# The four pairs of weight buffers of a two-layer encoder at four places modulo 512 bytes

## The chip, the cores and the metric

One core of one Trainium2 chip runs the whole program. The metric is the device time of one execution in microseconds, the less the better. Times before are 2304.95 and 2302.07 us, median 2303.51 us.

## The reference, cut to what matters

An encoder of two layers over 256 tokens of width 2048, all in float32. Layer 0 mixes tokens with gated linear attention, layer 1 with grouped-query attention; each then has a squared-ReLU MLP of width 8192 and a gate by a per-layer embedding.

```python
for i in range(DEPTH):
    u = rms_norm(h, g_pre_mix[i])
    mix = gla_mixer(u, ...) if i % 2 == 0 else gqa_mixer(u, ...)
    h = h + rms_norm(mix, g_post_mix[i])
    m = squared_relu_mlp(rms_norm(h, g_pre_mlp[i]), w_mlp_up[i], w_mlp_down[i])
    h = h + rms_norm(m, g_post_mlp[i])
    gate = sigmoid(h @ w_ple_gate[i])
    h = h + rms_norm(gate * (p[i] @ w_ple_proj[i]), g_ple[i])
```

## The kernel before, in words

Every large product is made in float32r with each operand cut into a high and a low part, and three terms are added up: high by high, high by low, low by high. X (128 partitions, 16 slices of 512 elements) holds the current input, in each slice 256 elements of high parts and then 256 of low parts. H, of the same shape, holds the input of the second product of a stage.

`WeightStream` brings the weights. A chunk is 128 x 1024 float32 (two slices of 128 rows by 512 columns). SP's queue loads it into one of four `raw` buffers, ACT casts it to a high part `whi` (L91), and DVE subtracts to get the low part `wlo` (L92). `whi` and `wlo` have four buffers each (NSPLIT = 4) of 4096 bytes per partition, taken in turn, so the ACT cast of chunk i waits until the matmuls of chunk i - 4 have read its buffer. A few chunks have a destination of their own (`W.dest`) in X, H or a small tile and don't take part in the rotation.

`gemm_b` (L373, L378) makes up, og and the first q and k products: the weights are the stationary operand, X streams. A chunk is 16 matmuls in turn of 512 columns (`whi` against both halves of X) and of 256 (`wlo` against X's high half). `gemm_a` (L300 to L302) makes the others: X or H is the stationary operand and the weights stream, 12 matmuls of 512 columns a chunk: high by `whi`, high by `wlo`, low by `whi`. `gemm_out` is `gemm_a` with its last group of columns in two passes (L339 to L341), the second in matmuls of 256 columns.

Tiles lie one after another in SBUF, in the order in which pools and tags are first used. In the pool `base`: ident (512 bytes per partition), cols, mhalf and ones (512 together), h (16384), X (32768). Then `wpool`: four `raw`, four `whi`, four `wlo`, 4096 bytes each. So modulo 512 all of these lie at X's place, and so does every slice of 128 or 512 elements in them. Then `sm` (small tiles), 19360 bytes up to `mem`, so that the tiles of `mem` (m2 and e4, among them `lrw`, v, qT, kT and prT) lie 416 bytes past X's place modulo 512. Then pools of single stages, and `L1`, which begins with a tile `gap` of 24 floats so that H lies at X's place again; kvlow, PT and other tiles of `L1` follow H.

Of the kernel before, what the change touches and what calls it, by code (L numbers as in the profile page):

```python
# [10 lines left out]
F32 = mybir.dt.float32  # L11
F32R = mybir.dt.float32r
# [5 lines left out]
P = 128  # L18
# [36 lines left out]
CH = KC * 512  # L55


class WeightStream:


    def __init__(self, nc, pool, nraw, nsplit):
        self.nc, self.pool, self.nraw, self.nsplit = nc, pool, nraw, nsplit
        self.chunks = []
        self.raw = {}
        self.split = {}
        self.nload = 0
        self.ndone = 0
        self.pos = 0
        self.on_load = {}
        self.todo = []  # L70
        self.dest = {}
        self.live = 0

    def add(self, ap, kt, n):
        self.chunks.append((ap, kt, n))
# [14 lines left out]
    def _cut(self, hi, lo, raw):  # L90
        self.nc.scalar.copy(hi, raw)  # L91
        self.todo.append(lambda: self.nc.vector.tensor_sub(lo, raw, hi.bitcast(F32)))  # L92

    def parts(self, i):

        kt = self.chunks[i][1]
        return [(k, k + 1) for k in range(kt)] if i == 0 else [(0, kt)]
# [6 lines left out]
    def _split(self, lows=True):  # L104
        i = self.ndone
        _, kt, n = self.chunks[i]
        raw = self.raw.pop(i)
        m = kt * n
        if i in self.dest:
            hi, lo = self.dest[i]  # L110
            if len(hi.shape) == 3:
                self._cut(hi, lo, raw[:, :m].rearrange("p (k n) -> p k n", k=kt))
                self.split[i] = (hi, lo)
                self.ndone += 1
                return
        else:
            hi = self.pool.tile([P, CH], F32R, tag="whi", name=f"whi{i}", bufs=self.nsplit)
            lo = self.pool.tile([P, CH], F32R, tag="wlo", name=f"wlo{i}", bufs=self.nsplit)
            self.live += 1
        for j, k in self.parts(i):  # L120
            self._cut(hi[:, j * n:k * n], lo[:, j * n:k * n], raw[:, j * n:k * n])
        if lows:
            self.lows()
        self.split[i] = (hi[:, :m].rearrange("p (k n) -> p k n", k=kt),
                         lo[:, :m].rearrange("p (k n) -> p k n", k=kt))
        self.ndone += 1
# [24 lines left out]
def kernel(ctx, tc, a, out):  # L151
# [657 lines left out]
        sl = drive(gemm_a(X, 4, v_evac, name="v"), plan, sl)  # L809

    L1 = ctx.enter_context(tc.tile_pool(name="L1", bufs=1))
    L1.tile([P, 24], F32, name="gap")
    H = L1.tile([P, KT, 512], F32R, name="H")

    def load_PT(i):
# [122 lines left out]
    with tc.tile_pool(name="att", bufs=1) as ap_:  # L938
# [166 lines left out]
        for g in range(4):  # L1105
            b = 8 * (g + 1) + ATT_LAG
# [80 lines left out]
```

## Time and profile before

| | us |
|---|---|
| the two runs | 2304.95, 2302.07 |
| their median | 2303.51 |
| the profiled execution | 2302.45 |
| its span, first to last instruction | 2300.7 |
| TensorE busy in the span | 2279.2 |
| VectorE (DVE) busy | 1421.7 |
| ScalarE (ACT) busy | 1215.2 |

Consecutive matmuls overlap in the trace: the time between the starts of two of them is shorter than the duration of one. How fast TensorE goes is therefore read from starts in the timeline, not from durations.

### The profile page before, as it was taken

Reading aid. Unit: us, or ns where it says so; the run is one execution under the profiler, and the core shown is the slowest. Engines: PE = TensorE matmul, PEld = TensorE weight load, DVE = VectorE, ACT = ScalarE, POOL = GpSimd, SP = SyncE. Lnnn points to the kernel's source line nnn. Section 1 sums busy time; section 2 is a strip of 40 time slices with the busy share of each in tenths; the row PEclk is TensorE's granted clock in tenths of the full one; section 3 lists DMA queues with packets and bytes.
Section 4 is the critical chain, followed back from the end, with each engine's and each line's share of the span. In section 5 each row is a group of like instructions: output and inputs, shape, how many; then the busy total and the mean of one; then the engine's idle time right before and its main releaser. Section 6 shows DMA issues by size and latency. Waiting matters only on the chain.

```text
span 2300.7 us, 31255 instructions
## 1 busy us (share of the span) xinstructions
PE 2279.2 (99%) x11956; PEld 1957.1 (85%) x11956; DVE 1421.7 (62%) x1920; ACT 1215.2 (53%) x1884; POOL 37.2 (2%) x58
## 2 busy tenths in 40 slices
PE   8999999999999999999999999999999999999998
PEld 7888888988888888888888888888888888888887
DVE  6888765664564565556667677665455455455565
ACT  6666554654453454455456565555455355355453
POOL 0000000000000000000000010000000000000000
PEclk9999999999999999999999999999999999999999
DMA  8555665665666665666565644666666666666654
GB/s 282 165 147 147 202 192 192 193 191 194 189 189 193 190 191 192 192 190 192 194 215 160 180 143 156 202 187 192 193 191 190 194 187 191 194 190 192 211 174 147
DMA packets 223783, 431.75 MB, mean 188 GB/s; under 512 B 15696, under 2 KB 16720, under 8 KB 222864
## 3 DMA queue, kind: packets, MB, share of 16 engines
q1 hardware_dynamic: 221328, 421.23, 59.5%
q10 hardware_dynamic: 2304, 8.52, 1.0%
q8 instruction: 93, 1.52, 0.3%
q14 instruction: 58, 0.48, 0.1%
HBM read 427.60 MB, written 2.10 MB: 187 GB/s over the span
## 4 chain that ended last, share of the span: by engine, by line
PE 94%; DVE 3%; ACT 1%; issue 1%; DMA 0%; SPq 0%; DVEq 0%; POOLq 0%; POOL 0%; ACTq 0%
PE u L373 20%; PE u L378 11%; PE d L302 9%; PE d L300 9%; PE d L301 9%; PE og L373 3%; PE g L301 2%; PE g L302 2%; PE g L300 2%; PE og L378 1%; PE q L302 1%; PE q L300 1%; PE q L301 1%; DVE wlo L92 1%; PE ao L302 1%
## 5 line engine op out<-in xcount | busy, mean ns | idle before, releaser
L92 DVE TENSOR_TENSOR wlo<-raw,whi 128x1024 fp32r<-128x1024 f32 (+1 forms) x770 | 937.7, 1221 | 731.7 <-ACT whi L91 729.6
L91 ACT CAST whi<-raw 128x1024 fp32r<-128x1024 f32 (+1 forms) x770 | 807.8, 1052 | 842.1 <-PE d L302 338.5
L373 PE MATMUL u<-X,whi 128*128 128x512 f32 x2048 | 711.0, 392 | 0.0
L378 PE MATMUL u<-X,wlo 128*128 128x256 f32 x2048 | 570.9, 280 | 0.0
L373 PEld LDWEIGHTS u<-X,whi 128*128 128x128 f32 x2048 | 383.0, 187 | 83.5
L378 PEld LDWEIGHTS u<-X,wlo 128*128 128x128 f32 x2048 | 386.1, 189 | 0.4
L302 PE MATMUL d<-whi,H 128*128 128x512 f32 x960 | 373.6, 389 | 0.0
L301 PE MATMUL d<-wlo,H 128*128 128x512 f32 x960 | 373.6, 389 | 0.0
L300 PE MATMUL d<-whi,H 128*128 128x512 f32 x960 | 373.4, 389 | 0.0
L302 PEld LDWEIGHTS d<-whi,H 128*128 128x128 f32 x960 | 180.2, 188 | 37.6
L300 PEld LDWEIGHTS d<-whi,H 128*128 128x128 f32 x960 | 180.2, 188 | 37.4
L301 PEld LDWEIGHTS d<-wlo,H 128*128 128x128 f32 x960 | 180.2, 188 | 37.3
L373 PE MATMUL og<-X,whi 128*128 128x512 f32 x256 | 89.6, 396 | 0.0
L300 PE MATMUL g<-whi,X 128*128 128x512 f32 x192 | 75.3, 392 | 0.0
L302 PE MATMUL g<-whi,X 128*128 128x512 f32 x192 | 74.8, 389 | 0.0
L301 PE MATMUL g<-wlo,X 128*128 128x512 f32 x192 | 74.7, 389 | 0.0
L378 PE MATMUL og<-X,wlo 128*128 128x256 f32 x256 | 71.2, 278 | 0.0
L373 PEld LDWEIGHTS og<-X,whi 128*128 128x128 f32 x256 | 48.0, 188 | 11.3
L417 ACT COPY u_c<-u 128x256 f32<-128x256 f32 x128 | 46.8, 366 | 17.5 <-PE u L378 17.5
L373 PE MATMUL q<-X,whi 128*128 128x512 f32 x128 | 46.5, 414 | 6.1 <-ACT whi L91 5.3
L300 PE MATMUL v<-whi,X 128*128 128x512 f32 x128 | 51.3, 401 | 0.0
L300 PE MATMUL q<-whi,X 128*128 128x512 f32 x128 | 50.8, 397 | 0.0
(428 smaller groups left out, 2984.9 us busy)
## 6 DMA issues: line engine op xcount, KB each, us to landing
raw<-in_w_mlp_up SPq DMA_DIRECT2D x256, 512.0 KB, 3.7
raw<-in_w_mlp_down SPq DMA_DIRECT2D x256, 512.0 KB, 3.8
raw<-in_gla_w_in SPq DMA_DIRECT2D x95, 512.0 KB, 4.0
raw<-in_w_ple_gate SPq DMA_DIRECT2D x64, 512.0 KB, 4.2
raw<-in_attn_w_in SPq DMA_DIRECT2D x48, 512.0 KB, 4.1
raw<-in_gla_w_out SPq DMA_DIRECT2D x32, 512.0 KB, 3.9
raw<-in_attn_w_out SPq DMA_DIRECT2D x32, 512.0 KB, 4.4
raw<-in_w_ple_proj SPq DMA_DIRECT2D x7, 512.0 KB, 5.3
```

The costliest lines, as they stand in the source:

```text
L91: self.nc.scalar.copy(hi, raw)
L92: self.todo.append(lambda: self.nc.vector.tensor_sub(lo, raw, hi.bitcast(F32)))
L300: mm(ps[g][t], xh, hi[:, k], start=K == 0, stop=False)
L301: mm(ps[g][t], xh, lo[:, k], start=False, stop=False)
L302: mm(ps[g][t], xl, hi[:, k], start=False, stop=K == nk - 1)
L373: mm(ps[f], hi[:, k, f * P:(f + 1) * P], op[:, K, :], start=K == 0, stop=K == 15, skip_group_check=True)
L378: mm(ps[f][:, T:], lo[:, k, f * P:(f + 1) * P], op[:, K, :T], start=False, stop=K == 15, skip_group_check=True)
L417: nc.scalar.copy(cr[:parts], ps[:parts, T:])
```

## The change

The eight buffers of the rotation get a tag each, with one buffer. A new method `homes` hands them out: pair b = turn modulo 4, where `turn` counts the chunks that take part in the rotation. At its first call it makes all eight in a fixed order, with three tiles in between that nobody writes or reads: 448 bytes, then whi0, wlo1, whi2, wlo2; 64 bytes, then wlo0, whi1, wlo3; 64 bytes, then whi3. Modulo 512 from X's place, (high, low) then lie at (448, 0) for pair 0, (0, 448) for pair 1, (448, 448) for pair 2 and (64, 0) for pair 3. All that lies behind `wpool` moves by 576 bytes. The tile `gap` ahead of H shrinks from 96 to 32 bytes, so H and the tiles behind it move by 512.

```diff
+        self.turn = 0
+        self.first = {}
...
+    def homes(self):
+
+        def new(nm):
+            return self.pool.tile([P, CH], F32R, tag=nm, name=nm, bufs=1)
+        if self.turn == 0:
+            for nm, pad in (("whi0", 448), ("wlo1", 0), ("whi2", 0), ("wlo2", 0),
+                            ("wlo0", 64), ("whi1", 0), ("wlo3", 0), ("whi3", 64)):
+                if pad:
+                    self.pool.tile([P, pad // 4], F32, tag="gap" + nm, name="gap" + nm, bufs=1)
+                self.first[nm] = new(nm)
+        b = self.turn % self.nsplit
+        self.turn += 1
+        return [self.first.pop(nm, None) if nm in self.first else new(nm) for nm in (f"whi{b}", f"wlo{b}")]
...
-            hi = self.pool.tile([P, CH], F32R, tag="whi", name=f"whi{i}", bufs=self.nsplit)
-            lo = self.pool.tile([P, CH], F32R, tag="wlo", name=f"wlo{i}", bufs=self.nsplit)
+            hi, lo = self.homes()
...
-    L1.tile([P, 24], F32, name="gap")
+    L1.tile([P, 8], F32, name="gap")
```

## Rows read from the trace of the kernel before

**Rows 1.** The page: busy time by engine; TensorE's clock in 40 slices, in tenths.

```profile
PE 2279.2 (99%) x11956; PEld 1957.1 (85%) x11956; DVE 1421.7 (62%) x1920; ACT 1215.2 (53%) x1884; POOL 37.2 (2%) x58
...
PEclk9999999999999999999999999999999999999999
```

**Rows 2.** The page: shares of the chain that ended last, by engine.

```profile
PE 94%; DVE 3%; ACT 1%; issue 1%; DMA 0%; SPq 0%; DVEq 0%; POOLq 0%; POOL 0%; ACTq 0%
```

**Rows 3.** Waits of TensorE: who waited for whom, total us, times, longest us.

```profile
PE q L373 <- ACT whi L91: 5.3, 2, 5.2
PE sc L706 <- DVE kcb L699: 3.7, 3, 1.9
PE k L373 <- DVE qk_s L418: 1.9, 1, 1.9
PE xt L426 <- DVE h L457: 0.9, 1, 0.9
PE q L373 <- DVE X L240: 0.8, 1, 0.8
PE v L301 <- DVE wlo L92: 0.2, 1, 0.2
```

**Rows 4.** Timeline, MLP's second product: start us, duration us, what; 16 distances apart.

```profile
1044.68 0.39 PE L300 MATMUL d<-whi,H 128*128 128x512 f32 x1
...
1048.31 0.39 PE L301 MATMUL d<-wlo,H 128*128 128x512 f32 x1
```

**Rows 5.** Timeline, MLP's first product (30 pairs), then the second's first ten distances.

```profile
1025.06 0.39 PE L373 MATMUL u<-X,whi 128*128 128x512 f32 x1
1025.29 0.28 PE L378 MATMUL u<-X,wlo 128*128 128x256 f32 x1
...
1035.45 0.39 PE L373 MATMUL u<-X,whi 128*128 128x512 f32 x1
...
1035.80 0.39 PE L300 MATMUL d<-whi,H 128*128 128x512 f32 x1
...
1038.11 0.39 PE L301 MATMUL d<-wlo,H 128*128 128x512 f32 x1
```

**Rows 6.** Timeline, second pass of the last columns: 19 distances of 256-column matmuls.

```profile
1112.00 0.28 PE L339 MATMUL d<-whi,H 128*128 128x256 f32 x1
...
1114.28 0.28 PE L340 MATMUL d<-wlo,H 128*128 128x256 f32 x1
```

**Rows 7.** Whole span, instructions on whi, then on wlo: PE, PEld, DVE, ACT; clock; DMA.

```profile
0.00:2300.70 2300.70, 2021.00 (x6304) 1173.98 (x6304) 937.65 (x770) 807.82 (x770) 1.00 0.61 188
...
0.00:2300.70 2300.70, 1425.94 (x4432) 835.70 (x4432) 937.65 (x770) 1.00 0.61 188
```

**Rows 8.** Timeline of ACT and DVE in the MLP's second product; idle time and releaser in brackets.

```profile
1044.20 1.05 ACT L91 CAST whi<-raw 128x1024 fp32r<-128x1024 f32 x1 [1.67 <-PE d L302]
1046.92 1.05 ACT L91 CAST whi<-raw 128x1024 fp32r<-128x1024 f32 x1 [1.67 <-PE d L302]
...
1045.29 1.22 DVE L92 TENSOR_TENSOR wlo<-raw,whi 128x1024 fp32r<-128x1024 f32 x1 [1.49 <-ACT whi L91]
```

**Rows 9.** Timeline, attention's output product, six distances of 256-column matmuls.

```profile
1320.82 0.28 PE L1078 MATMUL op<-prT,vn 128*128 128x256 f32 x1
...
1321.52 0.60 PE L1064 MATMUL pp<-ident,pr 128*128 128x128 f32 x4
```

**Rows 10.** Timeline, gate's low-rank product: 16 matmuls in one row, and the next.

```profile
54.89 3.87 PE L772 MATMUL lr<-X,lrw 128*64 128x512 f32 x16
58.60 0.39 PE L373 MATMUL q<-X,whi 128*128 128x512 f32 x1
```

**Rows 11.** Timeline, gated stage's og product: twelve pairs, and six pairs later.

```profile
227.84 0.40 PE L373 MATMUL og<-X,whi 128*128 128x512 f32 x1
...
232.08 0.40 PE L373 MATMUL og<-X,whi 128*128 128x512 f32 x1
...
283.47 0.39 PE L373 MATMUL og<-X,whi 128*128 128x512 f32 x1
...
285.55 0.39 PE L373 MATMUL og<-X,whi 128*128 128x512 f32 x1
```

**Rows 12.** The page: costliest groups, count | busy us, mean ns | idle us before and releaser.

```profile
L91 ACT CAST whi<-raw 128x1024 fp32r<-128x1024 f32 (+1 forms) x770 | 807.8, 1052 | 842.1 <-PE d L302 338.5
```

## The prediction

> **What bounds the kernel now.** I read the page first: busy times, clock and the chain that ended last. [...] Then its waits: together under 14 us in the whole span, nearly all in the first stages [rows 3]. So nothing that feeds TensorE sets the end. What sets it is the distance from the start of one matmul to the start of the next. A duration in a trace can't show that, because consecutive matmuls overlap, so I took starts from the timeline.
>
> In the MLP's second product 16 distances take 1048.31 - 1044.68 = 3.63 us, 226.9 ns each [rows 4]. [...] All of these have every operand at X's place modulo 512: base holds 1024 + 16384 bytes ahead of X, X itself, four raw, four high and four low buffers are multiples of 512, and H has been put there by the 96-byte gap.
>
> The matmuls that read a weight buffer of the rotation are 6304 (high) and 4432 (low), 10,736 together [rows 7]. [...]
>
> **The change, part by part.** *Homes in place of a shared rotation.* The gap tiles are never written and issue nothing; no instruction is added or taken away on any engine or DMA queue. Chunk i took the slot of chunk i - 4, and `turn % 4` gives the same. The ACT cast still waits for the last matmul on the old contents, as now [rows 8]. If separate tags made that wait one chunk longer, there is cover: casts start 1046.92 - 1044.20 = 2.72 us apart, cast and subtraction end 2.27 us after the start of the cast (1.05 us, then DVE at 1045.29 for 1.22), and the buffer is needed three chunks, about 8.2 us, after it came free [rows 8]. That leaves 5.9 us, two chunks. Without that cover each chunk would wait up to 2.3 us; I take 0.
>
> *Cast and subtraction at other addresses.* 1.05 and 1.22 us may move a little; the two together would have to grow beyond the 2.72 us of a chunk on either engine before TensorE notices. 0.
>
> *Everything behind the weight pool moves.* The gaps add 448 + 64 + 64 = 576 bytes, and H's gap shrinks by 64, so H moves by 512 and stays at X's place, with all that follows it in its pool. The small tiles and the work tiles of the attention and the gated stage move by 64 modulo 512. Some 300 matmuls read them; at 5 ns each that is under 2 us. 0.
>
> *The places of the pairs.* Pair 0 has its high half 64 bytes below X's place, pair 1 its low half, pair 2 both, pair 3 its high half 64 bytes above. The trace of before has no weight buffer at such a place. Its nearest rows have operands elsewhere by 96 or 416 bytes. Below: the attention's output product, weights and moving operand at 416, one weight in three at 0: six distances in 1321.52 - 1320.82 = 0.70 us, 116.7 ns [rows 9], 3.3 ns less than the 120.0 of the same shape at equal places. Above: the gate's low-rank product, X streaming against weights at 416 and 160: 16 distances in 58.60 - 54.89 = 3.71 us, 231.9 ns [rows 10], 5.0 ns more than 226.9, though with half the weight columns, so it is not quite the same shape. Over 10,736 matmuls the bounds are -35 and +54 us.
>
> Which value? Both rows are 32 bytes off any 64-byte boundary of X's place (416 = 6.5 x 64), while all the new places are whole multiples of 64. What the rows show may be a matter of such a boundary, which the change does not touch. Also, the spacing depends on more than places: in the gated stage, with the same operands at the same places as in rows 5, twelve pairs take 232.08 - 227.84 = 4.24 us, 353.3 ns a pair instead of 346.3 [rows 11]; and at the switch from the first to the second product the distances wander (the first ten take 1038.11 - 1035.80 = 2.31 us, 231 each) before they hold at 226.9 [rows 5]. A rhythm that settles by itself, at one value through hundreds of matmuls while ACT, DVE and DMA write other buffers, speaks for a fixed turn of access and not for collisions between two particular addresses. I take 0, with both bounds kept for the range.
>
> [...]
>
> *Sum.* 2302.45 us (the profiled execution: 2300.7 of span and 1.75 around it) + 0 = 2302.5, and the median of the runs stands 1.1 us above that execution: 2303 us.
>
> **The rivals.** *B, slower: the rhythm settles anew at each change of pair.* Place: each border between two chunks, about 769 of them (770 casts [rows 12]). Price: the settling above, 2.31 - 10 x 0.2269 = 0.041 us, times 769 = +32 us: 2335 us. For it: the rhythm does depend on where it starts [rows 5]. Against: now a chunk border costs nothing, and 16 equal distances in rows 4 run over one (a chunk has 12). It decides from the point where pairs at different places have different resting phases.
>
> *C, slower: a worse rhythm throughout.* The gated stage's 353.3 ns instead of 346.3 is 3.5 ns per matmul: +38 us, 2340 us; with the 5.0 ns of rows 10 it would be +54, 2356 us. For it: the rhythm of rows 11 holds by itself with nothing amiss on any engine, so a second resting state exists. Against: later in the same stage six pairs take 285.55 - 283.47 = 2.08 us, 346.7 ns each [rows 11]; the dearer rhythm had been left again.
>
> *D, faster: what rows 9 show.* 3.3 ns on all four pairs: -35 us, 2267 us; if half of the pairs gain, 2285 us. For it: rows 9 have mixed places and are the quickest of their shape. Against: six matmuls at a time, which may be settling and not a resting rhythm.
>
> [...]
>
> **How the numbers follow.** A, no change in the spacing: 0.50. B 0.16, C 0.12, D 0.19, E 0.03. A change of over 2% (46 us, about what a measurement of this kernel can tell from no change) needs 4.3 ns on each of the 10,736 matmuls. Slower by that much: a third of C (towards rows 10) and a quarter of B (a settling that takes longer than the one seen), 0.04 + 0.04 = 0.08. Faster by that much: E, and 0.03 of D for places that suit better than those of rows 9: 0.06. Within 2%: 0.86. The likeliest case alone is 2303 us, 2297 to 2309. The range reaches down to rows 9 on all pairs and up to the rhythm of rows 11 on all, 2268 to 2341; outside lie E, 0.03 of D, 0.04 of C and 0.04 of B, and some of the rest at their ends, under 0.2.
>
> **What would show it.** In the changed kernel's timeline the second product should keep 226.9 ns from start to start for each of the four chunks in turn, and the first product 346.3 a pair. [...] The mean durations of these groups, 389 and 392 with 280 ns now, would move with them. The prediction is wrong if a shift of 64 bytes changes which accesses meet: then a period of four chunks appears in the starts. A wait on the new homes would show as TensorE waiting for DVE's or ACT's cast in the MLP stages, where it now waits for nothing.

## The result: 1.1% slower, by the spacing of the matmuls alone

The changed kernel takes 2327.65 us (2326.61 to 2328.69) against 2303.51 us: ratio 1.011, interval 1.0093 to 1.0127. Its span is 2326.9 us, 26.2 us more than before.

The page of the changed kernel, busy time by engine, shares of the chain, and the groups of the MLP's two products (count | busy us, mean ns):

```profile
PE 2305.9 (99%) x11956; PEld 1955.7 (84%) x11956; DVE 1422.7 (61%) x1920; ACT 1212.1 (52%) x1884; POOL 37.2 (2%) x58
...
PE 95%; DVE 3%; ACT 1%; issue 1%; DMA 0%; SPq 0%; DVEq 0%; POOLq 0%; POOL 0%; ACTq 0%
...
L388 PE MATMUL u<-X,whi 128*128 128x512 f32 x2048 | 715.0, 395 | 0.0
L393 PE MATMUL u<-X,wlo 128*128 128x256 f32 x2048 | 570.6, 280 | 0.0
...
L315 PE MATMUL d<-whi,H 128*128 128x512 f32 x960 | 379.2, 395 | 0.0
L316 PE MATMUL d<-wlo,H 128*128 128x512 f32 x960 | 378.2, 394 | 0.0
L317 PE MATMUL d<-whi,H 128*128 128x512 f32 x960 | 378.1, 394 | 0.0
```

Against [rows 1, 2] TensorE is busy 26.7 us longer and idle 0.5 us less, ACT and DVE are busy within 3.1 us of before, and the chain is TensorE's as before. The matmuls of the second product last 394 to 395 ns instead of 389, with no idle time before them.

The waits of TensorE are those of [rows 3], short and in the first stages, and ACT's casts start 2.79 us apart instead of the 2.72 of [rows 8]: they follow TensorE. The changed kernel's longest waits (us in total, times, longest us), then two rows of ACT's timeline:

```profile
PE q L388 <- ACT whi L93: 5.7, 2, 5.4
PE sc L721 <- DVE kcb L714: 2.6, 3, 1.7
PE k L388 <- DVE qk_s L433: 2.0, 1, 2.0
...
1061.07 1.05 ACT L93 CAST whi<-raw 128x1024 fp32r<-128x1024 f32 x1 [1.75 <-PE d L317]
1063.86 1.05 ACT L93 CAST whi<-raw 128x1024 fp32r<-128x1024 f32 x1 [1.74 <-PE d L317]
```

Where the time is shows in starts. A matmul's spacing is the distance from its start to the next one's; in the first product it is given for a pair of matmuls, one of 512 columns (high) and one of 256 (low). From here on each kernel is measured over the same two long stretches: 240 distances within the second product (first quarter of the MLP in layer 0), and 120 pairs within the first product (its second quarter). The timeline of before, then of after (start us, duration us); the last two rows of after are 120 pairs of the first product's last quarter in layer 1:

```profile
517.85 0.39 PE L300 MATMUL d<-whi,H 128*128 128x512 f32 x1
...
572.24 0.39 PE L300 MATMUL d<-whi,H 128*128 128x512 f32 x1
...
615.96 0.39 PE L373 MATMUL u<-X,whi 128*128 128x512 f32 x1
...
657.56 0.39 PE L373 MATMUL u<-X,whi 128*128 128x512 f32 x1
```

```profile
519.61 0.39 PE L315 MATMUL d<-whi,H 128*128 128x512 f32 x1
...
575.36 0.39 PE L315 MATMUL d<-whi,H 128*128 128x512 f32 x1
...
619.85 0.39 PE L388 MATMUL u<-X,whi 128*128 128x512 f32 x1
...
661.97 0.40 PE L388 MATMUL u<-X,whi 128*128 128x512 f32 x1
...
2067.10 0.39 PE L388 MATMUL u<-X,whi 128*128 128x512 f32 x1
...
2108.57 0.39 PE L388 MATMUL u<-X,whi 128*128 128x512 f32 x1
```

Second product: 54.39 us before, 55.75 after, that is 226.6 and 232.3 ns a matmul. First product: 41.60 us before, 42.12 after, 346.7 and 351.0 ns a pair; in the last quarter only 345.6. Summed over all starts of the trace by product, after against before: the second product +15.9 us, the first +4.1, all others together +6.0: 26.0 of the 26.2 us. The +6.0 are +7.3 for the other products with streaming weights, +0.6 for the others with stationary ones, and -1.8 for the rest. The second product's weights stream past H and pay in every quarter, 231.9 to 232.2 ns a matmul there against 226.7; the first product's weights are stationary under X and hardly pay.

### The profile page after: what moved, and what is told of

It is laid out like the page before. It is cut to its first block, busy times and chain, and to the rows that moved or that the text cites. A ratio compares the mean times of both kernels' runs of the same rounds, so it can differ in the third digit from the quotient of the medians.

```text
span 2326.9 us, 31255 instructions
## 1 busy us (share of the span) xinstructions
PE 2305.9 (99%) x11956; PEld 1955.7 (84%) x11956; DVE 1422.7 (61%) x1920; ACT 1212.1 (52%) x1884; POOL 37.2 (2%) x58
## 4 chain that ended last, share of the span: by engine, by line
PE 95%; DVE 3%; ACT 1%; issue 1%; DMA 0%; SPq 0%; DVEq 0%; POOLq 0%; POOL 0%; ACTq 0%
PE u L388 20%; PE u L393 10%; PE d L315 10%; PE d L317 10%; PE d L316 10%; PE og L388 3%; PE g L315 2%; PE g L316 2%; PE g L317 2%; PE q L315 1%; PE og L393 1%; PE q L317 1%; PE q L316 1%; PE k L388 1%; PE go L315 1%; PE ao L315 1%
## 5 line engine op out<-in xcount | busy, mean ns | idle before, releaser
L388 PE MATMUL u<-X,whi 128*128 128x512 f32 x2048 | 715.0, 395 | 0.0
L393 PE MATMUL u<-X,wlo 128*128 128x256 f32 x2048 | 570.6, 280 | 0.0
L388 PEld LDWEIGHTS u<-X,whi 128*128 128x128 f32 x2048 | 384.6, 188 | 87.8
L393 PEld LDWEIGHTS u<-X,wlo 128*128 128x128 f32 x2048 | 384.6, 188 | 0.4
L315 PE MATMUL d<-whi,H 128*128 128x512 f32 x960 | 379.2, 395 | 0.0
L317 PE MATMUL d<-whi,H 128*128 128x512 f32 x960 | 378.1, 394 | 0.0
L388 PE MATMUL og<-X,whi 128*128 128x512 f32 x256 | 89.0, 394 | 0.0
L393 PE MATMUL og<-X,wlo 128*128 128x256 f32 x256 | 71.3, 278 | 0.0
L388 PEld LDWEIGHTS og<-X,whi 128*128 128x128 f32 x256 | 48.1, 188 | 10.7
L388 PE MATMUL q<-X,whi 128*128 128x512 f32 x128 | 46.2, 412 | 6.8 <-ACT whi L93 5.7
```

The costliest lines, as they stand in the source:

```text
L315: mm(ps[g][t], xh, hi[:, k], start=K == 0, stop=False)
L317: mm(ps[g][t], xl, hi[:, k], start=False, stop=K == nk - 1)
L388: mm(ps[f], hi[:, k, f * P:(f + 1) * P], op[:, K, :], start=K == 0, stop=K == 15, skip_group_check=True)
L393: mm(ps[f][:, T:], lo[:, k, f * P:(f + 1) * P], op[:, K, :T], start=False, stop=K == 15, skip_group_check=True)
```

## The experiments

Three theories. **P**: the distance of the weights from X and H modulo 512 sets the spacing. **B**: the rhythm settles anew at each change of pair, and the place itself costs nothing. **H** (a theory here, not the tile): the new homes cost it. Except where a diff says otherwise, a kernel differs from the changed one in the list of gaps (the bytes ahead of each home), and in H's gap, which keeps H at X's place; each diff but one is against the changed kernel, and the two lines that a new list of gaps replaces stand in the first diff only. A ratio is the time over that of the kernel before, run alongside.

**All pairs at (0, 0), with the new homes.**

```diff
-            for nm, pad in (("whi0", 448), ("wlo1", 0), ("whi2", 0), ("wlo2", 0),
-                            ("wlo0", 64), ("whi1", 0), ("wlo3", 0), ("whi3", 64)):
+            for nm, pad in (("whi0", 0), ("whi1", 0), ("whi2", 0), ("whi3", 0),
+                            ("wlo0", 0), ("wlo1", 0), ("wlo2", 0), ("wlo3", 0)):
...
-    L1.tile([P, 8], F32, name="gap")
+    L1.tile([P, 24], F32, name="gap")
```

> Homes as in the changed kernel, but all four pairs at (0, 0), X's place, and H's gap back at 96 bytes. Theory P (the places of the buffers set the spacing of the matmuls): 2303 us within 4, 226.8 ns per matmul in the second product and 346.7 ns per pair in the first, as before. Theory H (a tag and a home for each buffer costs the time, through waits or another order): 2325 to 2330 us, as the changed kernel.

2302.53 us against 2302.32, ratio 1.0001 (0.9992 to 1.0010). The timeline:

```profile
518.33 0.39 PE L315 MATMUL d<-whi,H 128*128 128x512 f32 x1
...
572.73 0.39 PE L315 MATMUL d<-whi,H 128*128 128x512 f32 x1
...
616.44 0.39 PE L388 MATMUL u<-X,whi 128*128 128x512 f32 x1
...
658.04 0.39 PE L388 MATMUL u<-X,whi 128*128 128x512 f32 x1
```

226.7 and 346.7 ns, as before. H falls: tags and homes cost nothing that the interval, 0.1%, can tell.

**All pairs at (448, 448).**

```diff
+            for nm, pad in (("whi0", 448), ("whi1", 0), ("whi2", 0), ("whi3", 0),
+                            ("wlo0", 0), ("wlo1", 0), ("wlo2", 0), ("wlo3", 0)):
...
-    L1.tile([P, 8], F32, name="gap")
+    L1.tile([P, 40], F32, name="gap")
```

> All four pairs at (448, 448), H at X's place: no change of place from chunk to chunk. Theory P, each pair by itself: what chunks of pair 2 show in the changed kernel holds throughout, 233.0 ns in the second product (before: 226.8) and 352.5 ns per pair in the first (before: 346.7): 4992 x 6.2 + 2560 x 5.8 ns = +46 us, 2349 us. Theory B (the rhythm settles anew at each change of pair, the place itself costs nothing): no change of pair is left, so 2303 us within 4, with 226.8 and 346.7 ns.

2342.15 us, ratio 1.0172 (1.0157 to 1.0187). The timeline:

```profile
520.32 0.39 PE L315 MATMUL d<-whi,H 128*128 128x512 f32 x1
...
576.32 0.39 PE L315 MATMUL d<-whi,H 128*128 128x512 f32 x1
...
621.06 0.40 PE L388 MATMUL u<-X,whi 128*128 128x512 f32 x1
...
663.46 0.40 PE L388 MATMUL u<-X,whi 128*128 128x512 f32 x1
```

233.3 and 353.3 ns, with no change of place from chunk to chunk. B as the whole cause falls. The total is 7 us below what P gave. By starts of the trace the products with streaming weights lost 27.6 us and not 31.0 (v lost 0.1, q 1.5), those with stationary weights 13.4 and not 14.8, and all else became 2.5 us shorter; the second product alone lost 18.6 us, the first 13.2.

The spacing holds right through a chunk, though ACT is busy for only 23.7 and DVE for 24.5 of the 56.0 us: the 240 distances repeat one pattern of six, 1400 ns together. And the sign turns within the same kernel. In the last pass of the second product the matmuls are 256 columns long; first the weights come from the moved buffers, then from chunks kept in X's tile, which has not moved:

```profile
1129.88 0.28 PE L354 MATMUL d<-whi,H 128*128 128x256 f32 x1
...
1133.62 0.28 PE L354 MATMUL d<-whi,H 128*128 128x256 f32 x1
...
1135.00 0.28 PE L354 MATMUL d<-X,H 128*128 128x256 f32 x1
...
1137.88 0.28 PE L354 MATMUL d<-X,H 128*128 128x256 f32 x1
```

33 distances from the moved buffers take 113.3 ns each, 24 from X's tile 120.0; in the kernel before both parts have 120.0 [rows 6]. So the spacing goes with the tile that is read, and at one and the same place the sign goes with the length: 6.7 ns less for 256 streaming columns, 6.7 ns more for 512.

**All pairs at (448, 0).**

```diff
+            for nm, pad in (("whi0", 448), ("whi1", 0), ("whi2", 0), ("whi3", 0),
+                            ("wlo0", 64), ("wlo1", 0), ("wlo2", 0), ("wlo3", 0)):
...
-    L1.tile([P, 8], F32, name="gap")
+    L1.tile([P, 24], F32, name="gap")
```

> All four pairs at (448, 0). Theory P: 232.2 ns in the second product (+5.4), 346.3 ns per pair in the first (-0.4): 4992 x 5.4 - 2560 x 0.4 ns = +26 us, 2329 us; if the first product's chunks of this pair were held up by their neighbours (341.6 ns stands in the og product), 2560 x -5 ns = -13 us instead, 2317 us. Theory B: 2303 us within 4.

2318.31 us, ratio 1.0068 (1.0051 to 1.0084). The timeline:

```profile
513.94 0.40 PE L315 MATMUL d<-whi,H 128*128 128x512 f32 x1
...
570.21 0.40 PE L315 MATMUL d<-whi,H 128*128 128x512 f32 x1
...
614.28 0.39 PE L388 MATMUL u<-X,whi 128*128 128x512 f32 x1
...
655.08 0.39 PE L388 MATMUL u<-X,whi 128*128 128x512 f32 x1
```

234.5 ns, the dearest of the second product, and 340.0 ns a pair, less than before. The total is that of P's second case, by which the chunks of this pair were held up by their neighbours in the changed kernel; but both terms are larger than it had them, by starts of the trace +33.6 us for all streaming weights and -16.5 for all stationary ones against +27 and -13, and partly cancel. The two products want opposite things. By product: the second +22.2 us, the first -13.3.

**All pairs at (0, 448).**

```diff
+            for nm, pad in (("whi0", 0), ("whi1", 0), ("whi2", 0), ("whi3", 0),
+                            ("wlo0", 448), ("wlo1", 0), ("wlo2", 0), ("wlo3", 0)):
...
-    L1.tile([P, 8], F32, name="gap")
+    L1.tile([P, 40], F32, name="gap")
```

> All four pairs at (0, 448). Theory P: 231.1 ns in the second product (+4.3), 349.4 ns per pair in the first (+2.7): 4992 x 4.3 + 2560 x 2.7 ns = +28 us, 2332 us. Theory B: 2303 us within 4.

2318.69 us, ratio 1.0068 (1.0053 to 1.0083); 228.9 and 350.0 ns. That is 13 us below P's 2332: its figures were read from chunks that stand between chunks of other places. The second product pays less than they say (+2.2 and not +4.3 ns a matmul), the first about what they say (+3.3 and not +2.7 a pair).

**All pairs at (64, 0)**, the low buffers first.

```diff
+            for nm, pad in (("wlo0", 0), ("wlo1", 0), ("wlo2", 0), ("wlo3", 0),
+                            ("whi0", 64), ("whi1", 0), ("whi2", 0), ("whi3", 0)):
```

> All four pairs at (64, 0): the last of the four places of the changed kernel, alone. Theory P (place alone, borders between pairs free): the changed kernel is the mean of the four kernels with one place each, so this one must be at 4 x 2327.65 - (2342.15 + 2318.31 + 2318.69) = 2331 us, with 232.7 ns in the second product as pair 3 shows in the changed kernel. Theory P+B (place, and in addition a price at each border): it is faster than that; at 2318 us, say, the borders would cost (2327.65 - 2324.3) = 3 us in all.

2326.95 us, ratio 1.0106 (1.0093 to 1.0120), 4 us below P's figure. The mean of the four kernels with one place each is (1.0172 + 1.0068 + 1.0068 + 1.0106) / 4 = 1.0104, the changed kernel 1.011 (1.0093 to 1.0127): borders cost no more than the intervals, some 4 us, can tell. By starts of the traces the mean of the four would give the second product +16.5 us and the first +0.8; the changed kernel has +15.9 and +4.1, so the change of places may cost the first product some 3 us. The timeline has something new. The first two rows are 120 pairs in the first product's first quarter, the last two the usual stretch in its second:

```profile
465.09 0.39 PE L388 MATMUL u<-X,whi 128*128 128x512 f32 x1
...
505.89 0.39 PE L388 MATMUL u<-X,whi 128*128 128x512 f32 x1
...
617.96 0.39 PE L388 MATMUL u<-X,whi 128*128 128x512 f32 x1
...
659.96 0.39 PE L388 MATMUL u<-X,whi 128*128 128x512 f32 x1
```

340.0 and 350.0 ns a pair, in one kernel, with the same operands at the same places: two resting rhythms. Over the eight quarters of both layers it is 340 in the first and fourth of each layer and 350 in the others.

**X, weights, H and what follows, all moved by 64 bytes; the distances are 0.**

The homes and H's gap are those of the kernel with all pairs at (0, 0).

```diff
+    base.tile([P, 16], F32, name="shift")
     X = base.tile([P, KT, 512], F32R, name="X")
```

> All four pairs at (0, 0) from X's place, but X, all weight buffers, H and all that follows lie 64 bytes further in memory (a tile of 64 bytes that nobody uses, ahead of X). Theory R (only the distance between the operands counts): 2303 us within 4, 226.8 ns and 346.7 ns per pair. Theory A (the address itself counts, modulo 128 or 512): as large a change as in the kernels with moved weights, 2315 us or more, or a gain as large.

2305.02 us, ratio 1.0012 (1.0002 to 1.0021): within the 4 us, though the interval leaves out 1. The timeline: two rows of the second product, then 120 pairs in the first product's first quarter:

```profile
518.60 0.39 PE L316 MATMUL d<-whi,H 128*128 128x512 f32 x1
...
573.00 0.39 PE L316 MATMUL d<-whi,H 128*128 128x512 f32 x1
...
460.67 0.40 PE L389 MATMUL u<-X,whi 128*128 128x512 f32 x1
...
503.07 0.40 PE L389 MATMUL u<-X,whi 128*128 128x512 f32 x1
```

The usual stretches have 226.7 and 346.7 ns; the first quarter of the first product in each layer holds 353.3 ns a pair, and the first product is 3.2 us longer for it. So in 14 of the 16 quarters of the two products the spacing follows the distance and not the address. In the other two a dearer rhythm holds at distance 0 too; what sets it off is not shown.

**All pairs at (64, 64).**

```diff
+            for nm, pad in (("whi0", 64), ("whi1", 0), ("whi2", 0), ("whi3", 0),
+                            ("wlo0", 0), ("wlo1", 0), ("wlo2", 0), ("wlo3", 0)):
```

> All four pairs at (64, 64): the weights 64 bytes above X's place instead of below. If the sign of the distance doesn't matter: 2342 us as with (448, 448), 233.3 ns and 353.3 ns per pair. If what counts is which operand is ahead, the two products (weights streaming in the one, stationary in the other) change roles: the second product differs from 233.3 ns and the first from 353.3 ns by several ns, and the total lies between 2290 and 2335 us.

2324.34 us, ratio 1.0096 (1.0082 to 1.0110); 228.9 and 353.3 ns. The sign matters for streaming weights (228.9 against 233.3 below X's place), not for stationary ones. The guess that the products change roles was half wrong.

**A place for each product.** Stationary weights at (448, 0), streaming ones at (0, 0), in the same buffers: each high buffer begins at 448, with a gap of 448 bytes ahead of it, and is 64 bytes longer; a streaming chunk starts 64 bytes into it. Each low buffer follows its high one, at 0. To make room, the tile S of the gated stage gets one buffer instead of two. The diff, in extracts, is against the kernel before.

```diff
+            n = CH + 16 if nm < "wl" else CH
...
+                self.pool.tile([P, 112], F32, tag=f"gap{b}", name=f"gap{b}", bufs=1)
...
+        o = 0 if i in self.low64 else 16
+        return hi[:, o:o + CH], lo
...
-            wchunks(a["w_mlp_up"][i], q * 2048, 2048)
+            wchunks(a["w_mlp_up"][i], q * 2048, 2048, low64=True)
...
-            S = sm.tile([P, 768], F32, tag="S", name=f"S{hd}", bufs=2)
+            S = sm.tile([P, 768], F32, tag="S", name=f"S{hd}", bufs=1)
```

> The high buffers are 64 bytes longer, and each chunk says where in its buffer it lies: chunks whose weights are stationary (up, og, first q and k) at (448, 0), all others at (0, 0). To make room, one buffer instead of two for the scores S of the gated stage. Theory P: 340.1 ns per pair in the first product, 226.8 ns in the second: 2560 x -6.6 ns = -17 us, 2286 us (ratio 0.9927). If the gain of (448, 0) were tied to what the second product does, or were lost at the switch of product: 2300 us or more.

2285.01 us, ratio 0.9928 (0.9915 to 0.9940), against 0.9927 expected. It beats the kernel before and the changed one. The timeline:

```profile
513.51 0.39 PE L321 MATMUL d<-whi,H 128*128 128x512 f32 x1
...
567.91 0.39 PE L321 MATMUL d<-whi,H 128*128 128x512 f32 x1
...
611.23 0.39 PE L394 MATMUL u<-X,whi 128*128 128x512 f32 x1
...
652.03 0.39 PE L394 MATMUL u<-X,whi 128*128 128x512 f32 x1
```

226.7 and 340.0 ns: the better of both. By product the first gained 13.3 us and og 2.1; the second changed nothing.

**All pairs at (256, 256).**

```diff
+            for nm, pad in (("whi0", 256), ("whi1", 0), ("whi2", 0), ("whi3", 0),
+                            ("wlo0", 0), ("wlo1", 0), ("wlo2", 0), ("wlo3", 0)):
...
-    L1.tile([P, 8], F32, name="gap")
+    L1.tile([P, 88], F32, name="gap")
```

> All four pairs at (256, 256), half of 512 bytes away. If the distance counts modulo 256 or less: 2303 us, 226.8 and 346.7 ns. If it counts modulo 512 and two streams meet only when they are close: lower than before in both products, below 2295 us. If any distance other than 0 unsettles the rhythm: 2318 us or more.

2301.99 us, ratio 1.0000 (0.9990 to 1.0010). The timeline:

```profile
519.45 0.39 PE L315 MATMUL d<-whi,H 128*128 128x512 f32 x1
...
573.85 0.39 PE L315 MATMUL d<-whi,H 128*128 128x512 f32 x1
...
617.57 0.39 PE L388 MATMUL u<-X,whi 128*128 128x512 f32 x1
...
659.17 0.39 PE L388 MATMUL u<-X,whi 128*128 128x512 f32 x1
```

226.7 and 346.7 ns, as at (0, 0). So 512 is not the measure: with both halves 256 bytes away it is as if nothing had moved.

**All pairs at (384, 0), at (480, 0), at (448, 64)**, three more distances; the diffs follow in this order.

```diff
+            for nm, pad in (("whi0", 384), ("whi1", 0), ("whi2", 0), ("whi3", 0),
+                            ("wlo0", 128), ("wlo1", 0), ("wlo2", 0), ("wlo3", 0)):
...
-    L1.tile([P, 8], F32, name="gap")
+    L1.tile([P, 24], F32, name="gap")
```

```diff
+            for nm, pad in (("whi0", 480), ("whi1", 0), ("whi2", 0), ("whi3", 0),
+                            ("wlo0", 32), ("wlo1", 0), ("wlo2", 0), ("wlo3", 0)):
...
-    L1.tile([P, 8], F32, name="gap")
+    L1.tile([P, 24], F32, name="gap")
```

```diff
+            for nm, pad in (("whi0", 448), ("whi1", 0), ("whi2", 0), ("whi3", 0),
+                            ("wlo0", 128), ("wlo1", 0), ("wlo2", 0), ("wlo3", 0)):
```

> All four pairs at (384, 0), the high halves 128 bytes below X's place. If the gain of the first product grows with the distance: under 340.1 ns per pair. If 64 bytes are the one good place: 345 ns or more. The second product is expected between 229 and 235 ns; total 2305 to 2335 us.

2322.86 us, ratio 1.0090 (1.0075 to 1.0105); 228.9 and 352.0 ns. The gain of 340.0 does not grow with the distance; at 128 bytes it is gone.

> All four pairs at (480, 0), the high halves 32 bytes below X's place. If a grain of 64 bytes counts, the spacing of the first product is that of neither (0, 0), 346.7 ns, nor (448, 0), 340.1 ns, but lies above both, as a block of 512 bytes then reaches into one grain more; if the distance counts smoothly, between 340 and 347 ns per pair. Total 2305 to 2335 us.

2328.77 us, ratio 1.0115 (1.0099 to 1.0130); 233.3 and 346.7 ns. The first product lies at the value of (0, 0), in the first quarter of each layer at 344.4: the reading above both values fails, and the smooth one, between 340 and 347, isn't borne out by a value that (0, 0) has as well.

> All four pairs at (448, 64). In the first product a high half below X's place gave -6.6 ns per pair, a low half below +3.3 ns; if the halves act by themselves and the low half's sign turns, the low half above gives a further gain: 335 to 338 ns per pair. If the place of the two halves to one another counts, no such gain: 345 ns or more. The second product between 229 and 235 ns; total 2300 to 2330 us.

2324.79 us, ratio 1.0101 (1.0086 to 1.0116); 231.1 and 353.3 ns. The halves don't act by themselves; in this kernel too the first product has two rhythms, 347 ns a pair in the odd quarters and 353 in the even ones.

All of them, each from its first and last start over the two stretches, with a second value where other quarters hold another:

| places (high, low) | second product, ns a matmul | first product, ns a pair | ratio |
|---|---|---|---|
| (0, 0), before | 226.6 | 346.7 | 1 |
| the four pairs in turn | 232.3 | 351.0 and 345.6 | 1.011 |
| (256, 256) | 226.7 | 346.7 | 1.0000 |
| (0, 448) | 228.9 | 350.0 | 1.0068 |
| (64, 64) | 228.9 | 353.3 | 1.0096 |
| (384, 0) | 228.9 | 352.0 | 1.0090 |
| (448, 64) | 231.1 | 353.3 and 347 | 1.0101 |
| (448, 448) | 233.3 | 353.3 | 1.0172 |
| (64, 0) | 233.3 | 350.0 and 340.0 | 1.0106 |
| (480, 0) | 233.3 | 346.7 and 344.4 | 1.0115 |
| (448, 0) | 234.5 | 340.0 | 1.0068 |
| by product | 226.7 | 340.0 | 0.9928 |

What is not settled: which accesses meet, if any do, and what decides which of two rhythms a stretch settles into. The runs give the spacing for eleven arrangements and no rule that yields them all.

## Why the prediction was wrong

**Right: what bounds the kernel, and that the spacing of the matmuls sets its time.** All but 0.2 us of the 26.2 us lie between starts of matmuls, and TensorE's idle time did not grow.

**Right: homes, casts and the other tiles at 0.** (0, 0) with the new homes gives ratio 1.0001, and moving everything by 64 bytes gives 1.0012. The cover that was named for the casts was not needed. (By its rows cast and subtraction end 1045.29 + 1.22 - 1044.20 = 2.31 us after the cast's start, not 2.27; nothing hangs on it.)

**Wrong: "I take 0" for the places of the pairs.** This term was +26 us in the traces, +24 us in the medians; the time lies in the whole range, 2268 to 2341, but far outside the likeliest case's own, 2297 to 2309. Three arguments carried it. The first was that the rows with operands at other places ([rows 9, 10]) lie off a boundary of 64 bytes, and that this boundary might be all they show. It was a guess for which no row spoke: (448, 448) and (64, 64) keep the boundary and give 1.0172 and 1.0096, while (480, 0) breaks it and gives the first product 346.7 ns, as at (0, 0), in three quarters of four, and the second product 233.3, as at (448, 448). The second was that the rhythm also varies at equal places ([rows 11]). That shows a second resting rhythm, and later runs have two at one place as well (340.0 and 350.0 ns at (64, 0)); it does not exclude that the place picks among them. The third was that a rhythm which settles by itself speaks for a fixed turn of access and not for collisions of two addresses. Both hold at once here: a spacing that rests, and that depends on the distance. The rows nearest to the change, -3.3 and +5.0 ns, had opposite signs and neither was 0. They were also of two lengths, [rows 9] of 256 columns and [rows 10] of 512, and in the products with streaming weights the sign does go with the length (-6.7 and +6.7 ns at (448, 448)); the prediction took them as two readings of one price. In the two long products the measured changes run from -3.3 ns (half of the 6.7 of a pair) to +7.8 ns a matmul, the 6.7 and 7.8 ns beyond the +5.0 of the rows. The totals, 2285 to 2342 us, lie within the bounds of -35 and +54 us that the prediction kept; that is partly luck, for those bounds put one price on all matmuls.

**The place counts by itself.** The prediction had noted that rows 6 and 9 differ by 3.3 ns, and yet its sum took one spacing at any place. With all pairs at (448, 448) ACT is busy for 1211.3 us and DVE for 1424.3, as before within 4 us, and the spacing in the second product goes from 226.7 to 233.3 ns. So the same shape does not have the same spacing at any place; whether two reads of TensorE meet, no run shows.

**The rivals.** B is not seen as a cost in the total (1.0104 for the mean of the four single places, 1.011 for all four in turn); some 3 us in the first product may be left for it, against the +32 us that it was priced at. C has the right sign and mechanism, a dearer spacing throughout, but not its size of +38 us and not in the product it was taken from: the streaming products paid, +5.7 ns a matmul in the second, and the first product hardly. D came true where it wasn't looked for: 3.3 ns a matmul is what (448, 0) gains in the products with stationary weights, and the few streaming matmuls of 256 columns gain too. The error of form was to apply one price to all 10,736 matmuls, where the two kinds, some 5000 each with streaming and with stationary weights (L388 and L393 are 2560 each), answer differently. E, that the equal places are what costs and that moved weights gain on every matmul, falls at all places that were tried; its chance of 0.03 counted on a saving per matmul that no run shows. In its place the runs showed 3.3 ns a matmul in the first product at (448, 0), 6.7 ns for 256 streaming columns at (448, 448), and in the second product nothing at all: its smallest spacing is the 226.7 ns of (0, 0).

**The signs that were named.** The prediction called itself wrong if a period of four chunks appeared in the starts, and it did. The starts of two neighbouring chunks of the changed kernel's second product, from pair 1 and then from pair 2, and of the chunk after them:

```profile
516.85 0.39 PE L315 MATMUL d<-whi,H 128*128 128x512 f32 x1
...
519.61 0.39 PE L315 MATMUL d<-whi,H 128*128 128x512 f32 x1
...
522.41 0.39 PE L315 MATMUL d<-whi,H 128*128 128x512 f32 x1
```

They last 2.76 and 2.80 us. The lengths repeat after eight chunks, which is two turns of the four pairs and one group of columns, and by pair the mean spacings are 232.2, 231.1, 232.9 and 232.7 ns for pairs 0 to 3; with all pairs at (448, 448) every chunk after the first of a quarter lasts 2.80 us. The pair with both halves moved stands out, as the dearest. The mean spacing went from 226.6 to 232.3 ns and the durations from 389 to 394 or 395 ns, while the 280 ns of the low matmuls in the first product stayed.

## What to carry to other kernels

Where TensorE runs back to back, measure the distance from start to start (226.6 ns here), not the duration (389 ns), and treat the distance between the weights' buffers and those of the other operand as a tuning parameter (256 bytes acted like 0 here, ratio 1.0000; 32, 64 and 128 did not, 1.0068 to 1.0172). Choose it for each kind and length of product by itself: the offset that gained 6.7 ns a pair under stationary weights cost 7.8 ns a matmul with streaming ones. When the nearest rows bracket zero, that is evidence of a dependence of unknown sign; it is no reason to take zero.

## What the runs showed that was not expected

The measured spacings come in steps. Where the pairs of the first product repeat one by one, 120 of them take 40.80, 41.60 or 42.40 us, 340.0, 346.7 or 353.3 ns a pair: a step is 0.80 us / 120 = 6.67 ns. With all pairs at one place each stretch repeats, to the ns or two, after a few matmuls, and what repeats is a whole number of these 6.67 ns in the stretches named here. In the second product three matmuls take 680.0, 686.7 or 700.0 ns (102, 103 or 105 steps), six take 1400.0 at (448, 448) and 1406.7 at (448, 0), nine take 2060.0 at (384, 0) and 2080.0 at (448, 64). In the first product one pair takes 51, 52 or 53 steps, two pairs take 700.0 ns, three 1060.0 at (448, 448), five 1760.0 at (384, 0). Matmuls of 512 and 256 columns at X's place differ by 226.7 - 120.0 = 106.7 ns, 0.417 ns a column; by that a step is the time of 16 columns, an estimate from 106.7 ns for 256 of them. What makes the steps, no run shows. And two spacings can hold for hundreds of matmuls with the same operands at the same places, 340.0 and 350.0 ns at (64, 0), 345.6 and 351.0 ns in the changed kernel; they change from one quarter of the MLP to the next, never within a stretch that was measured. At (64, 0) both layers show the same sequence of quarters; in the changed kernel five quarters hold 351 and the last three 345.6.
